# A one-core transformer layer: begun pairs in twos, more of them, and the second value bank in attention

## The chip, the core and the metric

The kernel runs on one core of a Trainium2 chip. The metric is the device time of one execution in microseconds (us); a kernel's time is the median of its runs. The engines are called TensorE (PE in the profile; PEld is its loading of weights), VectorE (DVE), ScalarE (ACT), GpSimd (POOL) and SyncE (SP, which issues DMAs here). SBUF is the memory on the chip that the engines work from; PSUM has eight banks, and matmuls sum into them.

## The reference

One layer of a diffusion backbone over 1024 latent tokens and 256 context tokens, width 1024, all in f32:

```python
x  = x  + 0.5 * ml[2] * swiglu(modulate(rms_norm(x,  norm1_g), ml[0], ml[1]), ffn1_w_in, ffn1_w_out)
cx = cx + 0.5 * mc[2] * swiglu(modulate(rms_norm(cx, norm1_g), mc[0], mc[1]), ffn1_w_in, ffn1_w_out)
hx, hc = modulate(rms_norm(x, norm2_g), ml[3], ml[4]), modulate(rms_norm(cx, norm2_g), mc[3], mc[4])
bg, cg, vc, q, k, v, gt = split(hx @ w_in)          # and the same of hc, for its keys and values
y_conv = bg * short_conv(cg * vc, conv_w)
o = attention(rope(rms_norm(q)), concat(k_ctx, rope(rms_norm(k))), concat(v_ctx, v))   # 8 heads, 2 for keys
x = x + ml[5] * (sigmoid(gt0) * (y_conv @ w_bc) + sigmoid(gt1) * (o @ w_ba)) @ w_out
x = x + 0.5 * ml[8] * swiglu(modulate(rms_norm(x, norm3_g), ml[6], ml[7]), ffn2_w_in, ffn2_w_out)
return rms_norm(x, final_g)
```

## The kernel before

**Precision.** Each f32 operand is split into a high part (a cast to fp32r by ScalarE) and a low part (the rest, a subtraction on VectorE). A product of two operands is three matmuls: high by high, high by low, low by high. `terms` issues these three for one of four blocks of the sum, `k`.

**Products by seven.** The big projections are done by the class `Winograd`. A pair of column blocks of the weights against the two halves of the tokens (`C0`, the first 512, and `C1`, the second 512) would take eight products of half-size blocks; seven products of sums of blocks suffice. Each product is 4 × 3 = 12 matmuls of 128x512, so a pair takes 84. The left factors are sums of weight blocks (made by GpSimd, tiles `sum`, or taken as fetched, tiles `raw`), split into tiles `wl` or `wh`. The right factors `r1` to `r7` are sums of the normalized input, each in four blocks `k`; `norm0` makes `r1` and `r2`, which need `C0` only, and `norm1` makes `r3` to `r7`, which need the normalized `C1`. The results are collected by VectorE in tiles `u`, `v`, `c` and `b`.

**Pairs begun ahead.** While `norm1` works, only products 1 and 2 can run. `start` therefore begins the first `n_ahead` pairs with these two products. For each pair it fetches a bank for product 1, has ScalarE copy the bank to `u`, runs one step of `norm1`, takes a second bank for product 2, and has VectorE add `u` and that bank into `c`. Then `put_aside` lets SyncE write `u` and `c` (tile `uc`, 512 KB) to DRAM (`ucd`). Later `fetch` brings them back one pair ahead, and `second` and `third` continue the pair with products 6, 7, 4, 5 and 3. The left factors of begun pairs are fetched first, all of them in front of those of the products that continue; the left blocks of a begun pair are fetched again later for its sums. Pairs that are not begun do all seven products in a row. Two stages use `start`: `mix`, the projection by `w_in` (20 pairs, `AH2` of them begun), and `fast`, the first matmul of the last FFN (22 pairs, `AH3` begun). The first FFN has a start of its own.

**Attention.** A `Unit` is one head with one half of the tokens; the 16 units alternate `C0` and `C1`. `scores` makes, for each of four blocks of 128 queries, the scores against 256 context keys and 2 × 512 latent keys; VectorE takes the maxima, ScalarE the exponentials. While the next unit's scores are made, `seconds` turns this unit's weights (`turn`, on TensorE) and sums the values (`values`, ten blocks of keys, 30 matmuls into one bank); at the end ScalarE copies the bank to `q` (`output`). Between them, matmuls of the convolution branch and of the merge fill in.

**Banks.** PSUM is given out by three rings: `ps_s` of five banks for products, scores and the rest, `ps_t` of two for transposes, and `ps_o` of one, which in attention holds the value sums. A bank comes free when all that read the tile before it have done so.

**Order.** The code is written in the order of its data, and a scheduler, which models the engines, decides in what order the instructions of each engine stand; an engine then works through its list in order. Each instruction waits for the ones that it depends on. All are issued by one helper, so the profile names line L90 for nearly all, and the tiles' names (with buffer numbers left out) tell them apart.

Of the kernel before, what the change touches and what calls it, by code (L numbers as in the profile page):

```python
# [9 lines left out]
F32 = mybir.dt.float32  # L10
# [8 lines left out]
P = 128  # L19
# [16 lines left out]
C0, C1, CC = ("l", 0, 512), ("l", 512, 512), ("c", 0, CT)  # L36

A_BUFS = 38
W_BUFS = 4
# [4 lines left out]
WAIT = 4  # L44
AH1, BY_HALF, WARM = 13, 8, 32
TOKENS_AT = 5
RESIDENT, AH2, AH3 = 2, 9, 9
SLOT = 1024


# [1 line left out]
def tile_dit_layer(  # L52
# [44 lines left out]
    act, dve, pool, pe, sp = (Engine(e) for e in (nc.scalar, nc.vector, nc.gpsimd, nc.tensor, nc.sync))  # L97
# [3 lines left out]
    wpool = ctx.enter_context(tc.tile_pool(name="wpool", bufs=5))  # L101
# [7 lines left out]
    def uniq(s):  # L109
        n_tiles[0] += 1  # L110
        return f"{s}_{n_tiles[0]}"
# [11 lines left out]
    def ps_s(n=512):  # L123
        return psum.tile([P, 512], F32, tag="s", name=uniq("ps"), bufs=5)[:, :n]
# [4 lines left out]
    def ps_o(n=512):  # L129
        return psum.tile([P, 512], F32, tag="o", name=uniq("po"), bufs=1)[:, :n]  # L130

    def matmul(out, w, x, start, stop, pinned=False, on=False):

        inst = pe.matmul(out, w, x, start=start, stop=stop, skip_group_check=on)
        if pinned:
            tc.keep_in_program_order(inst)
# [329 lines left out]
    def run(steps, n=None):  # L466

        if n is None:
            for _ in steps:
                pass  # L470
        else:
            for _ in range(n):
                next(steps, None)
# [18 lines left out]
    class Winograd:  # L492
# [192 lines left out]
            self.prefetch(4)  # L685
            return self.ready.pop(0)

        def terms(self, ps, w, i, k):
            r = self.r[i][k]
            wh, wl = (w[:, v, k * P : (k + 1) * P] for v in range(2))  # L690
            matmul(ps, wh, r[:, 0], start=k == 0, stop=False)
            matmul(ps, wh, r[:, 1], start=False, stop=False)
            matmul(ps, wl, r[:, 0], start=False, stop=k == 3)

        def product(self, i):
            w, ps = self.left(), ps_s()
# [12 lines left out]

        def start(self, norm):  # L710

            for i in range(self.n_ahead):
                t = wpool.tile([P, 2, 512], F32, tag="wh", name=uniq("uc"), bufs=W_BUFS)
                u, c = t[:, 0], t[:, 1]
                act.copy(out=u, in_=self.product(1))
                run(norm, 1)
                dve.tensor_add(out=c, in0=u, in1=self.product(2))
                self.put_aside(t)
            run(norm)
            self.fetch()  # L720

# [369 lines left out]
    for k in range(4):  # L1091
        if k % 2:
            half1.shifted(h0[k][:, 0], k, xh[k])
        else:
            dve.tensor_scalar(
                out=h0[k][:, 0], in0=xh[k], scalar1=gain1["l"][:, k : k + 1], scalar2=modl[:, k : k + 1],
# [3 lines left out]
    start = half1.start_by_half()  # L1100
# [58 lines left out]
    steps = all_later_mods()  # L1159
# [66 lines left out]
    for j in range(NH):  # L1226
        half1.side = side(j) if j >= SIDE_FROM else None
        u, c = half1.next_first()
# [117 lines left out]
    for i in range(KD):  # L1346
        u = atile("u")
# [5 lines left out]
        for ch, bg, gc in mixed():  # L1353
# [4 lines left out]
            for j in (0, 2):  # L1358
# [3 lines left out]
                    out=ya, in0=u[:, a + j - 1 : b + j - 1], scalar=col(f"w{j}", i), in1=ya, op0=ALU.mult, op1=ALU.add  # L1362
# [207 lines left out]
    class Unit:  # L1570
# [45 lines left out]

        def values(self, kt, pts):
            if kt == 0:
                self.po = ps_o()
            po = self.po  # L1620
            vh, vl = (v[:, self.g * HD : (self.g + 1) * HD] for v in v_tile(kt))
            matmul(po, vh, pts[:, 0], start=(kt == 0), stop=False)
            matmul(po, vh, pts[:, 1], start=False, stop=False)
            matmul(po, vl, pts[:, 0], start=False, stop=(kt == 9))
# [63 lines left out]
    u = units[0]  # L1688
# [57 lines left out]
    for ch in (C0, C1):  # L1746
        o = ch[1]
        for d in range(KD):
            w = load_cols(w_out[0], d * P)
            load(xs(d, ch), xd[d, :, o : o + 512])  # L1750
            ps = ps_s()
# [4 lines left out]
                out=xs(d, ch), in0=ps, scalar=modl[:, 40 + d : 41 + d], in1=xs(d, ch), op0=ALU.mult, op1=ALU.add  # L1756
# [12 lines left out]
        out=gf[:], in0=cols[:, voff["gf"] : voff["gf"] + 8], scalar1=math.sqrt(D), scalar2=None, op0=ALU.mult  # L1769
# [133 lines left out]
```

## Time and profile before

| what | value |
|---|---|
| median of three runs | 2644.59 us (2644.15 to 2645.6) |
| the profiled execution | 2648.45 us |
| its span in the profile | 2646.7 us, mean granted clock of TensorE 0.994 |
| TensorE busy | 2620.2 us, 99% of the span, 12,665 matmuls and transposes |
| VectorE busy | 2019.7 us, 76% |
| ScalarE busy | 1173.9 us, 44% |
| GpSimd busy | 549.7 us, 21% |
| `mix` begins, on TensorE | 879.24 us |
| attention | about 1456 to 1854 us |
| `fast` continues its first pair | about 2037 us |

The profile comes from one execution, and its times are counted from the start of its span. A line of the timeline gives the start of a group of like instructions, the time that it takes, engine, line, operation, output and inputs, shapes and count, and in brackets how long the engine stood idle before it and which instruction ended that. A line of a window gives its length, then the busy time of TensorE, its weight loads, VectorE, ScalarE and GpSimd with the number of instructions in brackets, then the granted clock of TensorE as a share of full speed, the share of DMA engines in use, and GB/s. Matmul ends are modelled, so that starts are the surer times.

### The profile page before, as it was taken

The numbers are of one execution on the slowest core, as the hardware profiler recorded it, in microseconds if no ns is written. First come the engines' busy times: TensorE is split into PE (matmuls) and PEld (weight loads), VectorE is DVE, ScalarE is ACT, GpSimd is POOL, SyncE is SP. The second block draws the span as 40 slices with busy tenths as digits, with TensorE's granted clock in tenths as the row PEclk, the third lists the DMA queues.
The fourth block names the chain that finished last, engine by engine and source line by source line (L and its number), as shares of the span: only waits on it lengthen the run. The fifth ranks groups of instructions, "written<-read, shape, count | busy, mean of one in ns | idle before, by whom it ended". The sixth has DMA issues, their size and how long they took to land.

```text
span 2646.7 us, 35358 instructions
## 1 busy us (share of the span) xinstructions
PE 2620.2 (99%) x12665; PEld 2180.4 (82%) x12665; DVE 2019.7 (76%) x3382; ACT 1173.9 (44%) x2321; POOL 549.7 (21%) x425
## 2 busy tenths in 40 slices
PE   8999999999999999999999999999999999999998
PEld 6888898888888777888888888888887888888888
DVE  5888876888897898877788676685457876666996
ACT  6533454433554632333355576674235333334553
POOL 0144101221010044332023112141001442321100
PEclk9999999999999999999999999999999999999999
DMA  8666465335973455242522532123525542327831
GB/s 322 203 211 195 140 214 168 113 120 204 319 170 115 136 171 169 98 133 78 204 73 91 88 88 64 33 49 105 161 81 178 185 155 86 98 76 281 197 84 64
DMA packets 367018, 378.40 MB, mean 143 GB/s; under 512 B 19431, under 2 KB 252025, under 8 KB 366841
## 3 DMA queue, kind: packets, MB, share of 16 engines
q1 hardware_dynamic: 357400, 357.22, 41.7%
q0 software_dynamic: 9440, 18.91, 4.3%
q8 instruction: 99, 1.62, 0.3%
q14 instruction: 79, 0.64, 0.1%
HBM read 306.26 MB, written 69.76 MB: 142 GB/s over the span
## 4 chain that ended last, share of the span: by engine, by line
PE 59%; DVE 2%; ACT 1%; issue 1%; DMA 0%; POOL 0%; SPq 0%; DVEq 0%; ACTq 0%; POOLq 0%
PE ps L90 49%; PE po L90 5%; PE pt L90 5%; DVE xb L90 0%; DVE y L90 0%; DVE r L90 0%; DMA c<-ucd 0%; DVE wl L90 0%; DVE rs_t L90 0%; ACT r L90 0%; DVE wc L90 0%; ACT pts L90 0%; POOL sum L90 0%; DVE pts L90 0%; ACT q L90 0%
## 5 line engine op out<-in xcount | busy, mean ns | idle before, releaser
L90 PE MATMUL ps<-r,wl 128*128 128x512 f32 x5196 | 1208.1, 392 | 10.8 <-DVE r L90 4.8
L90 PEld LDWEIGHTS ps<-r,wl 128*128 128x128 f32 x5196 | 976.0, 189 | 220.7 <-DVE r L90 6.7
L90 ACT CAST wl<-raw 128x512 fp32r<-128x512 f32 x287 | 177.7, 619 | 235.9 <-PE ps L90 189.2
L90 ACT CAST wl<-sum 128x512 fp32r<-128x512 f32 x218 | 134.2, 620 | 301.5 <-PE ps L90 244.9
L90 DVE TENSOR_TENSOR wl<-raw,wl 128x512 fp32r<-128x512 f32 x287 | 209.3, 731 | 62.2 <-ACT wl L90 60.8
L90 POOL TENSOR_TENSOR sum<-raw 128x512 f32<-128x512 f32 x55 | 81.0, 1472 | 657.1 <-DMA raw<-in_w_in_dram 208.5
L90 DVE TENSOR_TENSOR wl<-sum,wl 128x512 fp32r<-128x512 f32 x218 | 194.6, 894 | 23.2 <-ACT wl L90 22.0
L90 DVE TENSOR_TENSOR u<-u,ps 128x512 f32<-128x512 f32 x186 | 126.1, 679 | 39.2 <-PE ps L90 39.1
L90 DVE SCALAR_TENSOR_TENSOR macc<-rawm,silu_c,macc 128x512 f32<-128x512 f32 x178 | 144.5, 830 | 10.3 <-DMA rawm<-in_w_mod_dram 9.9
L90 POOL TENSOR_TENSOR sum<-raw,sum 128x512 f32<-128x512 f32 x55 | 79.0, 1437 | 323.5 <-DVE wl L90 318.0
L90 ACT CAST rh<-hid 128x512 fp32r<-128x512 f32 x132 | 82.0, 622 | 135.2 <-PE ps L90 108.1
L90 DVE TENSOR_TENSOR pts<-pt,pts 128x512 fp32r<-128x512 f32 x160 | 108.6, 686 | 42.5 <-ACT pts L90 40.6
L90 ACT CAST pts<-pt 128x512 fp32r<-128x512 f32 x160 | 93.3, 594 | 86.3 <-PE pt L90 82.6
L90 DVE TENSOR_REDUCE m<-ps 128x1 f32<-128x512 f32 (+1 forms) x192 | 110.2, 594 | 24.3 <-PE ps L90 20.1
L90 PE MATMUL ps<-rh,wl 128*128 128x512 f32 x360 | 122.8, 390 | 0.0
L90 PE MATMUL ps<-wh,r 128*128 128x512 f32 x384 | 120.7, 392 | 0.0
L90 ACT CAST wh<-raw 128x512 fp32r<-128x512 f32 (+1 forms) x85 | 68.0, 801 | 101.3 <-PE ps L90 79.2
L90 DVE TENSOR_TENSOR rl<-hid,rh 128x512 fp32r<-128x512 f32 x132 | 89.9, 684 | 27.0 <-ACT rh L90 18.2
L90 PE MATMUL po<-pts,vh 128*128 128x512 f32 x256 | 110.0, 435 | 0.2 <-ACT pts L90 0.2
L90 PE MATMUL ps<-kl,qs 128*128 128x512 f32 x384 | 104.1, 395 | 0.0
L90 PE MATMUL ps<-rh,wh 128*128 128x512 f32 x300 | 102.8, 389 | 0.0
L90 PE MATMUL ps<-y,wc 128*128 128x512 f32 x384 | 97.1, 392 | 0.2 <-DVE g L90 0.2
(318 smaller groups left out, 5080.8 us busy)
## 6 DMA issues: line engine op xcount, KB each, us to landing
raw<-in_ffn_w_in_dram SPq DMA_DIRECT2D x130, 512.0 KB
raw<-in_ffn_w_out_dram SPq DMA_DIRECT2D x72, 512.0 KB
raw<-in_w_in_dram SPq DMA_DIRECT2D x61, 512.0 KB
rawm<-in_w_mod_dram SPq DMA_DIRECT2D x104, 256.0 KB
hid<-hd SPq DMA_DIRECT2D x40, 512.0 KB
rawm<-in_w_mod_dram SPq DMA_DIRECT2D x32, 512.0 KB
ucd<-uc SPq DMA_DIRECT2D x29, 512.0 KB
ws<-in_ffn_w_out_dram POOLq DMA_DIRECT2D x26, 512.0 KB, 6.4
```

Source lines behind the costliest of these rows:

```text
L90: inst = getattr(self.engine, name)(*args, **kw)
```

## The change

There are three edits.

1. Twelve pairs are begun ahead in `mix` instead of nine, ten in `fast` instead of nine.
2. `start` begins pairs by twos. It takes the four left factors of two pairs and one bank for each, runs product 1 of both, has ScalarE copy both banks to `u`, and then runs product 2 into the same banks without clearing them (`begins=False`), so that a bank then holds the sum of both products. ScalarE copies that to `c`. The addition on VectorE is gone. In the first group of a stage the terms of both pairs are issued in turn for each `k`; in the others one chain follows the other.
3. In attention a unit of `C1` takes the bank of its value sums from `ps_s`, a unit of `C0` from `ps_o` as before.

```diff
-RESIDENT, AH2, AH3 = 2, 9, 9
+RESIDENT, AH2, AH3 = 2, 12, 10
...
-        def terms(self, ps, w, i, k):
+        def terms(self, ps, w, i, k, begins=True):
             r = self.r[i][k]
             wh, wl = (w[:, v, k * P : (k + 1) * P] for v in range(2))
-            matmul(ps, wh, r[:, 0], start=k == 0, stop=False)
-            matmul(ps, wh, r[:, 1], start=False, stop=False)
-            matmul(ps, wl, r[:, 0], start=False, stop=k == 3)
+            matmul(ps, wh, r[:, 0], start=begins and k == 0, stop=False, on=not begins)
+            matmul(ps, wh, r[:, 1], start=False, stop=False, on=not begins)
+            matmul(ps, wl, r[:, 0], start=False, stop=k == 3, on=not begins)
...
         def start(self, norm):
 
-            for i in range(self.n_ahead):
-                t = wpool.tile([P, 2, 512], F32, tag="wh", name=uniq("uc"), bufs=W_BUFS)
-                u, c = t[:, 0], t[:, 1]
-                act.copy(out=u, in_=self.product(1))
-                run(norm, 1)
-                dve.tensor_add(out=c, in0=u, in1=self.product(2))
-                self.put_aside(t)
+            for j in range(0, self.n_ahead, 2):
+                n = min(2, self.n_ahead - j)
+                self.prefetch(2 * n)
+                ws, ps = [self.ready.pop(0) for _ in range(2 * n)], [ps_s() for _ in range(n)]
+                ts = [wpool.tile([P, 2, 512], F32, tag="wh", name=uniq("uc"), bufs=W_BUFS) for _ in range(n)]
+                for i in (1, 2):
+                    steps = [(k, e) for k in range(4) for e in range(n)]
+                    for k, e in steps if j == 0 else sorted(steps, key=lambda s: s[1]):
+                        self.terms(ps[e], ws[2 * e + i - 1], i, k, i == 1)
+                    for e in range(n):
+                        act.copy(out=ts[e][:, i - 1], in_=ps[e])
+                    if i == 1:
+                        run(norm, n)
+                for t in ts:
+                    self.put_aside(t)
             run(norm)
             self.fetch()
...
         def values(self, kt, pts):
             if kt == 0:
-                self.po = ps_o()
+                self.po = ps_s() if self.ch == C1 else ps_o()
             po = self.po
```

The number of matmuls is the same. Three places show what moves; the names end in the tile's numbers, which differ between the kernels, and the part after the arrow is what is read.

TensorE where `mix` begins, before (`ps_1469`, `ps_1480` are product 1 of pairs 0 and 1, `ps_1476`, `ps_1484` product 2; `r1_1428` to `r1_1431` are the four blocks of `r1`, `r2_1442` on those of `r2`):

```order
L90 MATMUL ps_1469_8296<-r1_1428_8048,wl_1463_8281 128x512 x3
L90 MATMUL ps_1469_8296<-r1_1429_8053,wl_1463_8281 128x512 x3
L90 MATMUL ps_1469_8296<-r1_1430_8058,wl_1463_8281 128x512
L90 MATMUL ps_1476_8334<-r2_1442_8145,wl_1464_8284 128x512
L90 MATMUL ps_1480_8354<-r1_1428_8048,wl_1466_8289 128x512 x3
L90 MATMUL ps_1480_8354<-r1_1429_8053,wl_1466_8289 128x512 x3
L90 MATMUL ps_1480_8354<-r1_1430_8058,wl_1466_8289 128x512
L90 MATMUL ps_1469_8296<-r1_1430_8058,wl_1463_8281 128x512 x2
L90 MATMUL ps_1469_8296<-r1_1431_8063,wl_1463_8281 128x512
L90 MATMUL ps_1480_8354<-r1_1430_8058,wl_1466_8289 128x512 x2
L90 MATMUL ps_1480_8354<-r1_1431_8063,wl_1466_8289 128x512
L90 MATMUL ps_1484_8378<-r2_1442_8145,wl_1467_8292 128x512
```

The same place now, from the last block of product 1 on (`ps_1468` is the bank of pair 0, `ps_1469` that of pair 1):

```order
L90 MATMUL ps_1468_8295<-r1_1431_8063,wl_1463_8281 128x512
L90 MATMUL ps_1469_8296<-r1_1431_8063,wl_1466_8289 128x512
L90 MATMUL ps_1468_8295<-r1_1431_8063,wl_1463_8281 128x512 x2
L90 MATMUL ps_1469_8296<-r1_1431_8063,wl_1466_8289 128x512 x2
L90 MATMUL ps_1468_8295<-r2_1442_8145,wl_1464_8284 128x512 x3
L90 MATMUL ps_1468_8295<-r2_1443_8150,wl_1464_8284 128x512 x3
L90 MATMUL ps_1468_8295<-r2_1444_8155,wl_1464_8284 128x512 x3
L90 MATMUL ps_1468_8295<-r2_1445_8160,wl_1464_8284 128x512
L90 MATMUL ps_1485_8395<-r1_1428_8048,wl_1480_8381 128x512 x2
L90 MATMUL ps_1468_8295<-r2_1445_8160,wl_1464_8284 128x512 x2
L90 MATMUL ps_1469_8296<-r2_1442_8145,wl_1467_8292 128x512 x3
L90 MATMUL ps_1469_8296<-r2_1443_8150,wl_1467_8292 128x512 x3
```

Before, the two products of two pairs stood mixed in four banks. Now the blocks of product 1 of both pairs stand in front (the rows ahead of these read `r1_1428` to `r1_1430`), and product 2 of pair 0 follows into the bank that product 1 left.

TensorE at the end of the begun pairs in `mix`, before (`ps_1575` is the last begun product 2; `ps_1591`, `ps_1593`, `ps_1599`, `ps_1601` are products 6, 7, 4 and 5 of pair 0):

```order
L90 MATMUL ps_1575_8768<-r2_1445_8160,wl_1562_8702 128x512 x3
L90 MATMUL ps_1591_8806<-r6_1499_8439,wl_1568_8728 128x512 x2
L90 MATMUL ps_1593_8824<-r7_1497_8433,wl_1572_8748 128x512 x2
L90 MATMUL ps_1599_8850<-r4_1500_8443,wl_1574_8765 128x512 x2
L90 MATMUL ps_1601_8867<-r5_1498_8436,wl_1590_8803 128x512 x2
L90 MATMUL ps_1591_8806<-r6_1499_8439,wl_1568_8728 128x512
L90 MATMUL ps_1591_8806<-r6_1516_8506,wl_1568_8728 128x512 x3
L90 MATMUL ps_1591_8806<-r6_1533_8573,wl_1568_8728 128x512 x3
L90 MATMUL ps_1593_8824<-r7_1497_8433,wl_1572_8748 128x512
L90 MATMUL ps_1593_8824<-r7_1514_8500,wl_1572_8748 128x512 x3
L90 MATMUL ps_1593_8824<-r7_1531_8567,wl_1572_8748 128x512 x3
L90 MATMUL ps_1599_8850<-r4_1500_8443,wl_1574_8765 128x512
```

The same place now (`ps_1574` is product 2 of the twelfth pair, `ps_1600` and `ps_1602` are products 6 and 7 of pair 0):

```order
L90 MATMUL ps_1574_8812<-r2_1444_8155,wl_1572_8808 128x512 x3
L90 MATMUL ps_1574_8812<-r2_1445_8160,wl_1572_8808 128x512 x3
L90 MATMUL ps_1600_8911<-r6_1499_8452,wl_1596_8899 128x512 x2
L90 MATMUL ps_1602_8929<-r7_1497_8446,wl_1597_8902 128x512 x2
L90 MATMUL ps_1600_8911<-r6_1499_8452,wl_1596_8899 128x512
L90 MATMUL ps_1600_8911<-r6_1509_8480,wl_1596_8899 128x512 x3
L90 MATMUL ps_1600_8911<-r6_1531_8584,wl_1596_8899 128x512 x3
L90 MATMUL ps_1600_8911<-r6_1539_8606,wl_1596_8899 128x512 x3
```

Before, the four products of pair 0 stood mixed, their first blocks in front, and came after nine pairs. Now product 6 runs whole behind twelve pairs, with two matmuls of product 7 among it.

TensorE in attention at the end of a `C0` unit's values, before (`po_2420` is that unit's bank, `po_2479` the next unit's, of `C1`; `vc`, `vh`, `vl` are parts of the values, `pt` are turned weights, `ps_2458` scores):

```order
L90 MATMUL po_2420_13509<-pts_2453_13652,vl_2068_11534 128x512
L90 MATMUL pt_2469_13719<-ident_75,pl_2403_13429 128x128
L90 MATMUL pt_2469_13719<-ident_75,pl_2415_13485 128x128
L90 MATMUL pt_2469_13719<-ident_75,pl_2427_13541 128x128
L90 MATMUL pt_2469_13719<-ident_75,pl_2447_13620 128x128
L90 MATMUL po_2479_13766<-pts_2466_13696,vc_2069_11535 128x512 x3
L90 MATMUL po_2479_13766<-pts_2468_13710,vc_2069_11535 128x512
```

The same place now (`ps_2476` is the bank of the `C1` unit):

```order
L90 MATMUL po_2417_13518<-pts_2450_13661,vl_2065_11543 128x512
L90 MATMUL pt_2466_13728<-ident_75,pl_2400_13438 128x128
L90 MATMUL pt_2466_13728<-ident_75,pl_2412_13494 128x128
L90 MATMUL pt_2466_13728<-ident_75,pl_2424_13550 128x128
L90 MATMUL pt_2466_13728<-ident_75,pl_2444_13629 128x128
L90 MATMUL ps_2455_13676<-kc_2075_11559,qs_2451_13670 128x256 x2
L90 MATMUL ps_2455_13676<-kc_2075_11559,qs_2452_13671 128x256
L90 MATMUL pt_2474_13767<-ident_75,pl_2400_13438 128x128
L90 MATMUL pt_2474_13767<-ident_75,pl_2412_13494 128x128
L90 MATMUL pt_2474_13767<-ident_75,pl_2424_13550 128x128
L90 MATMUL pt_2474_13767<-ident_75,pl_2444_13629 128x128
L90 MATMUL ps_2476_13775<-pts_2463_13705,vc_2066_11544 128x512 x3
```

The `C1` unit's values now go to a bank of the ring, in which the scores (`ps_2455`, `ps_2479`) stand too, and scores and turns stand in front of its first value matmul.

## The prediction

> **What bounds the kernel now.** I read the page first, then TensorE's waits, then the timeline and the windows around each wait, then the chain.
>
> ```profile
> PE 2620.2 (99%) x12665; PEld 2180.4 (82%) x12665; DVE 2019.7 (76%) x3382; ACT 1173.9 (44%) x2321; POOL 549.7 (21%) x425
> ```
>
> The page's first part: TensorE (PE) is busy 99% of the span, so only its pauses, or a lower granted clock, can be won back while the matmuls stay 12,665. VectorE (DVE) at 76% is an average that hides stages in which it is full.
>
> ```profile
> PE ps L90 <- DVE r L90: 4.8, 5, 2.0
> PE ps L90 <- ACT r L90: 3.8, 4, 1.3
> ...
> PE ps L90 <- DVE wl L90: 2.0, 1, 2.0
> ...
> PE po L90 <- ACT q L90: 1.1, 4, 0.3
> ```
>
> TensorE's waits (sum, times, longest). The first three lines touch the operands `r`, the sums of the normalized input, and the weight parts `wl`; the last is the value bank in attention. Next, the price of one matmul when nothing is late, from the chain of waits:
>
> ```profile
> 1142.79 95.23 PE ps L90 x420
> ```
>
> 95.23/420 = 0.2267 us. With it every stall is priced as elapsed time less matmuls × 0.2267. The timeline of TensorE where the projection stage (`mix`) begins:
>
> ```profile
> 879.24 1.07 PE L90 MATMUL ps<-r,wl 128*128 128x512 f32 x4
> 881.11 0.98 PE L90 MATMUL ps<-r,wl 128*128 128x512 f32 x3 [0.81 <-DVE r L90]
> 883.23 9.60 PE L90 MATMUL ps<-r,wl 128*128 128x512 f32 x41 [1.14 <-ACT r L90]
> 892.66 0.95 PE L90 MATMUL pt<-ones,sq_acc 128*128 128x1 f32 x8
> ```
>
> 892.66 − 879.24 = 13.42 us for 4 + 3 + 41 = 48 matmuls, which take 10.88: **2.5 us lost** while the first operands come. Where the ninth begun pair ends and the pairs are continued:
>
> ```profile
> 937.61 3.63 PE L90 MATMUL ps<-r,wl 128*128 128x512 f32 x15
> 943.22 0.96 PE L90 MATMUL ps<-r,wl 128*128 128x512 f32 x3 [1.98 <-DVE r L90]
> 944.91 34.66 PE L90 MATMUL ps<-r,wl 128*128 128x512 f32 x139 [0.73 <-DVE r L90]
> 979.41 0.50 PE L90 MATMUL pt<-ones,sq_acc 128*128 128x1 f32 x4
> ```
>
> 41.80 us for 157 matmuls (35.59): **6.2 us lost**. And at the next lack of weights:
>
> ```profile
> 994.65 7.94 PE L90 MATMUL ps<-r,wl 128*128 128x512 f32 x33
> 1004.64 47.69 PE L90 MATMUL ps<-r,wl 128*128 128x512 f32 x202 [2.05 <-DVE wl L90]
> 1052.17 0.38 PE L90 MATMUL pt<-ident,rs_y 128*128 128x128 f32 x2
> ```
>
> 57.52 us for 235 (53.27): **4.2 us lost**. Where the last FFN's stage (`fast`) begins:
>
> ```profile
> 2036.72 6.93 PE L90 MATMUL ps<-r,wl 128*128 128x512 f32 x28
> 2044.36 1.25 PE L90 MATMUL ps<-r,wl 128*128 128x512 f32 x3 [0.70 <-ACT r L90]
> 2046.58 10.30 PE L90 MATMUL ps<-r,wl 128*128 128x512 f32 x36 [0.96 <-DVE r L90]
> 2057.50 4.71 PE L90 MATMUL ps<-r,wl 128*128 128x512 f32 x18 [0.62 <-ACT r L90]
> ```
>
> 20.78 us for 67 (15.19): **5.6 us lost**. The losses are larger than the waits named. The granted clock (the third number from the right) says why:
>
> ```profile
> 940.00:960.00 20.00, 17.29 (x63) 13.37 (x62) 16.34 (x18) 7.36 (x16) 10.22 (x7) 0.83 0.41 134
> 1000.00:1020.00 20.00, 17.95 (x73) 14.32 (x72) 16.49 (x21) 5.63 (x10) 10.47 (x8) 0.91 0.60 197
> 2040.00:2050.00 10.00, 8.25 (x25) 4.93 (x24) 8.11 (x12) 8.88 (x16) 3.20 (x3) 0.83 0.60 198
> ```
>
> The clock lost is (1 − 0.83) × 20 = 3.4 us, 0.09 × 20 = 1.8 and 0.17 × 10 = 1.7. Each follows waits of 0.7 to 2.05 us.
>
> So 13.0 us lie at place 1 (`mix`), 5.6 at place 2 (`fast`) and 1.1 in attention: 19.7 us are in play.
>
> **The change, part by part.**
>
> *Twelve pairs begun instead of nine, ten instead of nine.* A begun pair does 24 of its 84 matmuls ahead, 5.44 us. Products 6, 7, 4 and 5 need operands that VectorE makes meanwhile:
>
> ```profile
> 948.24 0.68 DVE L90 TENSOR_TENSOR r<-nt,r 128x512 fp32r<-128x512 f32 x1
> ```
>
> Pair 0's first products are issued by about 939 us (wait at 943.22), the last operands are ready near 949: about 10 us late. Three more pairs move that point 3 × 5.44 = 16.3 us back, while VectorE's work until then does not grow: the operands lead by some 6 us, and the 6.2 us stall goes. (Three pairs bring six weight parts, 6 × 0.68 = 4.1 us, less than the additions that go, below.) What is late next is the weights of pair 0, whose fetch stands on SP's queue behind the last puts-aside; a fetch takes about this long (chain):
>
> ```profile
> 987.59 4.21 DMA c<-ucd
> ```
>
> TensorE's waits named no fetch in these stretches, so the fetches are ahead; I take 0.2 us and keep 0 to 4.2, a whole one. At place 2 the 67 matmuls would have ended at 2036.72 + 15.19 = 2051.9, and the last operand came near 2057.5. One pair more moves the need to 2057.3, and VectorE and ScalarE have the time of the removed additions besides: I leave 0.8 us of the 5.6 and keep 0 to 5.6.
>
> *The sum of products 1 and 2 is made in the bank.* VectorE loses one addition for each begun pair, ScalarE (ACT) gains one copy (and three and one pairs more):
>
> ```profile
> L90 ACT COPY uc<-ps 128x512 f32<-128x512 f32 x31 | 17.8, 586 | 22.0 <-PE ps L90 21.8
> ```
>
> Nine additions, each 0.68 like the addition of the same size quoted above, are 6.1 us that leave a VectorE which is the late engine at place 1; ScalarE takes 24 copies × 0.586 = 14.1 us instead of 5.3 over 65 us, with its 7.36 us of 20 in the window from 940 as the nearest load. That is hidden, except in the first group. There product 2 adds onto the bank only after ScalarE copied it, and ScalarE is full with operands, without a pause, until the copy that before starts at:
>
> ```profile
> 887.42 0.59 ACT L90 COPY uc<-ps 128x512 f32<-128x512 f32 x1
> ```
>
> The first 24 matmuls are done before that; if the copy starts at 887.4 the second 24 start near 888.0 and end at 888.0 + 5.44 = 893.4, where 890.1 would be without loss: 3.3 us instead of 2.5. The wait is then some 2 us in one piece, of the kind that cost clock in three places above. I put half of 1.7 us on it, 0.85 (bounds 0 and 1.7). The wait for the copy stands at the head of TensorE's queue, and behind it wait all later chains; at later groups the second bank's twelve matmuls (2.7 us) cover the copy's 0.59.
>
> [...]
>
> *The stall at 1002.* It came when a weight part met a slow addition:
>
> ```profile
> 1002.84 1.75 DVE L90 TENSOR_TENSOR wl<-sum,wl 128x512 fp32r<-128x512 f32 x1
> ```
>
> Such additions (1.75 instead of 0.68 us) lie beside GpSimd's sums. After the change the pairs come in another phase; nothing removes this for certain, but VectorE enters the pairs without backlog. I leave 0.5 of the 4.2 us, and keep 0 to 4.2.
>
> *What gets worse.* A pair that was whole takes 84 × 0.2267 = 19.0 us, a continued one 60 × 0.2267 = 13.6, with nearly the same work on VectorE. The windows of four pairs, the first two continued, the last two whole:
>
> ```profile
> 1038.60:1052.30 13.70, 13.70 (x63) 11.31 (x62) 13.12 (x17) 3.12 (x5) 4.74 (x4) 1.00 0.42 135
> 1052.30:1066.00 13.70, 13.70 (x63) 11.35 (x62) 13.60 (x21) 3.84 (x7) 4.70 (x3) 1.00 0.60 211
> 1066.00:1085.00 19.00, 19.00 (x85) 15.76 (x84) 17.92 (x25) 7.16 (x12) 7.94 (x5) 1.00 0.40 131
> 1085.00:1104.10 19.10, 19.10 (x86) 15.79 (x86) 12.46 (x20) 6.71 (x12) 5.01 (x4) 1.00 0.25 78
> ```
>
> Continued pairs already fill 13.12 and 13.60 of 13.70 us. The first whole one has 17.92; without two weight parts and one addition (3 × 0.68) it is 15.9 in 13.6, 2.3 us short, and the next has 12.46 − 2.0 = 10.5 and catches up. Part of the shortage lies in work that TensorE doesn't wait for: 0.7 us, from 0 to 4.
>
> Four more pairs also put aside and fetch back 512 KB each and fetch one left part twice, 1.5 MB × 4 = 6 MB. In the windows above DMA is busy 0.25 to 0.60, so it hides; uncovered it would be in the queue wait counted already.
>
> *The value bank in attention.* Eight units take a bank of the ring of five. Before, a unit's first value matmul waited for the copy out of the single bank:
>
> ```profile
> 1498.71 0.59 ACT L90 COPY q<-po 128x512 f32<-128x512 f32 x1
> ...
> 1500.31 0.71 ACT L90 ACTIVATE pl<-ps,nm 128x512 f32<-128x512 f32 x1
> ```
>
> ```profile
> 1499.36 1.18 PE L90 MATMUL po<-pts,vc 128*128 128x512 f32 x4 [0.31 <-ACT q L90]
> ```
>
> The four waits of 1.1 us go, and 1.0 is my value. From above the bound is the stage's whole idle time, 398.00 − 395.95 = 2.05 us:
>
> ```profile
> 1456.00:1854.00 398.00, 395.95 (x2134) 330.34 (x2133) 265.66 (x550) 242.89 (x596) 89.44 (x85) 1.00 0.29 72
> ```
>
> From below it is a ring that runs short: 2 us, three exponentials of the row above (0.71 each).
>
> **Sum.** Place 1: left are 3.3 + 0.85 + 0.2 + 0.5 + 0.7 = 5.5, gain 13.0 − 5.5 = 7.5. Place 2: 5.6 − 0.8 = 4.8. Attention 1.0. Together 13.3 us, 0.50%. The profiled execution, 2648.45 us (span 2646.7), would become 2635.2. It lies 3.9 above the median of 2644.59; the median becomes **2631.3**.
>
> **The rivals.** A measurement of this kernel can tell 0.2%, 5.3 us, from no change.
>
> *Stalls only move.* VectorE, not the operands, is the bound of continued pairs, so its shortage shows at once: the 4.2 us stay, the 4 us of the pairs come in full, the first group takes 3.3 + 1.7: left 13.4 at place 1, gain −0.4; place 2 gives 4.8 and attention 1.0, together 5.4: 2639.2. If place 2 gives half, 2641.6. For it: 13.60 of 13.70. Against it: six additions fewer stand before this stretch, and 10.5 after it.
>
> *Slower: the ring runs dry in attention.* Each of the eight units holds one of five banks through its ten values, while four rounds of scores want two to three banks each. If each of the 8 × 4 = 32 rounds waits for one more exponential, 0.71 us, that is 22.7 us; less 13.3, +9.4: 2654.0. It decides from 13.3/32 = 0.42 us a round. For it: ring banks come free only behind ScalarE's exponentials. Against it: no wait for a `ps` bank is among the waits in attention, ScalarE is busy 242.89 of 398.00, and TensorE idles only 2.05. [...]
>
> *All goes.* Nothing new is late: 19.7 us, 2624.9.
>
> *No effect.* The scheduler already mixed the first two pairs' products, so twos may bring nothing, and the operands are late by something other than place in the order: 2644.6. Against it: the wait at 943.22 names `r`, and 16.3 us of other matmuls come in front of it.
>
> **Chances.** Forecast 0.68, stalls only move 0.20, slower 0.04, all goes 0.06, no effect 0.02. The predicted time is that of the forecast. Its own bounds: 2624.9 with everything gone; with the terms that are most open at their bad ends by half (2 of the 4 us of the pairs, 2 of the 4.2, half the clock, 1.4 at place 2) about 7 us are lost, 2638.3. Eight in ten: 2625.0 to 2640.5, which takes in most of the first rival. Faster by over 0.2% needs under 2639.3: the forecast, all goes, and half of the first rival, 0.84; within 0.2%: the other half and no effect, 0.12; slower 0.04.
>
> **What would show it.** Right: between the first group and pair 4 no wait for `r` longer than 0.3 us, granted clock 1.00 where it was 0.83; no addition `uc<-uc,ps` in these stages; in attention no wait for `ACT q`. The first group is right if it waits about 2 us for the copy `uc<-ps`. Wrong: waits for `DVE wl` after 1000 us with a clock under 0.95 (stalls only move); waits for `ACT pl` or `ACT pc` on `ps` in attention (the ring). The prediction is wrong if the time is over 2640.5, or if place 2 keeps more than 3 us.

## The result, and the profile after

The changed kernel takes **2635.68 us** (median of 6 runs, 2634.84 to 2637.66), the kernel before in the same comparison 2644.97 (6 runs). The ratio is 0.9961, 95% interval 0.9951 to 0.9971: about 9.3 us, 0.35% by the medians, faster. Forecast were 2631.3 us and 13.3 us of gain, range 2625.0 to 2640.5. The time lies inside the range; the gain is 70% of the one forecast. The profiled execution's span fell from 2646.7 to 2635.9 us, by 10.8.

The first part of the page after:

```profile
PE 2613.6 (99%) x12665; PEld 2178.3 (83%) x12665; DVE 1997.9 (76%) x3360; ACT 1180.8 (45%) x2343; POOL 543.7 (21%) x425
```

The count of matmuls is the same; VectorE did 22 instructions fewer and ScalarE 22 more. TensorE's waits (sum, times, longest):

```profile
PE ps L90 <- ACT uc L90: 1.8, 2, 1.1
PE pt L90 <- DVE pts L90: 1.7, 7, 0.4
...
PE ps L90 <- ACT r L90: 1.3, 1, 1.3
PE ps L90 <- ACT pc L90: 0.8, 1, 0.8
...
PE ps L90 <- DVE r L90: 0.4, 1, 0.4
```

`DVE r` fell from 4.8 to 0.4 us, `ACT r` from 3.8 to 1.3, and `ACT q` is gone. New are `ACT uc` (the copy out of the bank), `ACT pc` (an exponential) and, not shown, 0.6 us for `DVE nm`; the wait for `DVE pts` (turned weights in attention) rose from 0.7 to 1.7. Place 1 in TensorE's timeline, from the first matmul of `mix` on:

```profile
881.02 1.52 PE L90 MATMUL ps<-r,wl 128*128 128x512 f32 x6
882.89 0.98 PE L90 MATMUL ps<-r,wl 128*128 128x512 f32 x3 [0.35 <-DVE r L90]
884.81 3.70 PE L90 MATMUL ps<-r,wl 128*128 128x512 f32 x15 [0.94 <-DVE wl L90]
889.65 6.91 PE L90 MATMUL ps<-r,wl 128*128 128x512 f32 x29 [1.14 <-ACT uc L90]
896.40 0.95 PE L90 MATMUL pt<-ones,sq_acc 128*128 128x1 f32 x8
...
904.96 87.09 PE L90 MATMUL ps<-r,wl 128*128 128x512 f32 x383
991.89 0.50 PE L90 MATMUL pt<-ones,sq_acc 128*128 128x1 f32 x4
992.25 68.31 PE L90 MATMUL ps<-r,wl 128*128 128x512 f32 x300
1060.39 0.38 PE L90 MATMUL pt<-ident,rs_y 128*128 128x128 f32 x2
1060.53 19.75 PE L90 MATMUL ps<-r,wl 128*128 128x512 f32 x86
1080.68 4.62 PE L90 MATMUL ps<-r,wl 128*128 128x512 f32 x19 [0.40 <-DVE wl L90]
```

The first group: 53 matmuls from 881.02 to 896.40, 15.38 us against 53 × 0.2267 = 12.01, so 3.4 us are lost. From 904.96 to 1080 there is no stop: the 300 matmuls behind 992.25 take 1060.39 − 992.25 = 68.14 us, 300 × 0.2267 = 68.01. The stalls that stood at 943 and 1002 are both gone, and only 0.40 us is waited for in a later continued pair. The windows say the same of the clock (third number from the right), and give attention as a whole in the last line:

```profile
880.00:900.00 20.00, 17.57 (x79) 13.65 (x78) 15.68 (x34) 14.21 (x27) 0.00 (x0) 1.00 0.59 195
1000.00:1020.00 20.00, 20.00 (x90) 16.57 (x89) 19.90 (x31) 6.31 (x11) 7.29 (x5) 1.00 0.41 135
1070.00:1090.00 20.00, 19.60 (x87) 15.90 (x86) 20.00 (x28) 5.82 (x10) 7.29 (x5) 1.00 0.52 165
1435.00:1855.00 420.00, 416.68 (x2229) 347.58 (x2229) 275.23 (x571) 251.22 (x615) 89.45 (x85) 1.00 0.26 76
```

The clock is 1.00 in all, also from 1000 us on, where it was 0.91 before. VectorE is at 20.00 of 20.00 in the stretch with the 0.40 wait. In attention TensorE is idle 420.00 − 416.68 = 3.32 us; a window of the same length in the profile before was

```profile
1440.00:1860.00 420.00, 417.76 (x2236) 348.30 (x2235) 278.87 (x573) 252.13 (x615) 89.72 (x86) 1.00 0.30 76
```

2.24 us. Attention became 1.1 us worse by these windows. They match only to about 2 us (the first scores start at 1432.5 us now and at 1439.9 before); a window of the changed kernel from 1432 on has 3.58 us idle, 1.3 us more than before. Place 2:

```profile
2000.27 19.54 PE L90 MATMUL ps<-r,wl 128*128 128x512 f32 x85
2020.52 39.77 PE L90 MATMUL ps<-r,wl 128*128 128x512 f32 x174 [0.70 <-ACT uc L90]
```

85 matmuls take 19.27 us and had 2020.52 − 2000.27 = 20.25, so 1.0 us is lost, around one wait of 0.70 for the copy.

### The profile page after: what moved, and what is told of

It reads as the page before. It is cut to its first block, busy times and chain, and to the rows that moved or that the text cites. A ratio compares the mean times of both kernels' runs of the same rounds, so it can differ in the third digit from the quotient of the medians.

```text
span 2635.9 us, 35385 instructions
## 1 busy us (share of the span) xinstructions
PE 2613.6 (99%) x12665; PEld 2178.3 (83%) x12665; DVE 1997.9 (76%) x3360; ACT 1180.8 (45%) x2343; POOL 543.7 (21%) x425
## 4 chain that ended last, share of the span: by engine, by line
PE 93%; DVE 3%; ACT 1%; DMA 1%; issue 1%; SPq 0%; POOL 0%; DVEq 0%; ACTq 0%
PE ps L90 80%; PE pt L90 8%; PE po L90 6%; DMA rawm<-in_w_mod_dram 1%; DVE wl L90 0%; DVE xb L90 0%; DVE macc L90 0%; DVE m L90 0%; DVE y L90 0%; ACT x L90 0%; DVE pts L90 0%; ACT r L90 0%; DMA hd<-u 0%; DMA mcol<-mrow 0%; ACT wl L90 0%
## 5 line engine op out<-in xcount | busy, mean ns | idle before, releaser
L90 DVE TENSOR_REDUCE m<-ps 128x1 f32<-128x256 f32 (+1 forms) x192 | 110.9, 596 | 29.7 <-PE ps L90 28.8
L90 POOL TENSOR_TENSOR sum<-sum,raw 128x512 f32<-128x512 f32 x55 | 88.2, 1603 | 5.6 <-PE ps L90 3.9
```

What stands on the lines that cost most here:

```text
L90: inst = getattr(self.engine, name)(*args, **kw)
```

## The experiments

Each is one kernel against the kernel before on the same chip; the ratio is its time over that kernel's. Beside its time stands what TensorE lost by place in its profiled execution: the sum, over all matmul starts, of the time to the next start beyond the median for that kind of matmul (512 columns: 227 ns). By this measure the kernel before lost 2.7, 6.4, 4.3 and 6.2 us where the prediction's rows gave 2.5, 6.2, 4.2 and 5.6. "First group" is the start of `mix`, "pair 0" the stretch where the begun pairs end and pair 0 is continued, "later pairs" what follows it in `mix`, "place 2" the start of `fast`. "Attention" is TensorE's idle time in a window of 420 us (– where none was read).

| kernel | us (before on that chip) | ratio, 95% interval | first group | pair 0 | later pairs | place 2 | attention |
|---|---|---|---|---|---|---|---|
| before | 2644.97 | | 2.7 | 6.4 | 4.3 | 6.2 | 2.24 |
| changed | 2635.68 (2644.97) | 0.9961, 0.9951 to 0.9971 | 3.5 | 0.0 | 0.8 | 1.1 | 3.32 |
| ahead_only | 2637.07 (2646.68) | 0.9960, 0.9946 to 0.9973 | 2.7 | 0.0 | 1.7 | 2.6 | – |
| twos_only | 2643.12 (2646.68) | 0.9986, 0.9978 to 0.9995 | 3.5 | 7.2 | 0.5 | 3.9 | – |
| bank_only | 2648.06 (2646.68) | 1.0005, 0.9996 to 1.0014 | 2.7 | 4.5 | 4.5 | 6.2 | 3.32 |
| no_bank | 2635.95 (2646.68) | 0.9959, 0.9946 to 0.9971 | 3.5 | 0.0 | 1.3 | 1.1 | 3.60 |
| ahead_10 | 2640.92 (2647.60) | 0.9977, 0.9967 to 0.9986 | 3.5 | 2.5 | 5.0 | 1.1 | – |
| ahead_14 | 2636.07 (2647.60) | 0.9960, 0.9947 to 0.9972 | 3.5 | 0.0 | 1.2 | 1.1 | – |
| first_four_banks | 2636.44 (2647.60) | 0.9961, 0.9949 to 0.9974 | 2.0 | 0.0 | 0.7 | 3.1 | – |
| add_on_vector | 2639.30 (2647.60) | 0.9969, 0.9958 to 0.9981 | 2.0 | 0.9 | 2.8 | 2.7 | – |
| four_in_mix | 2633.11 (2646.69) | 0.9950, 0.9937 to 0.9962 | 2.0 | 0.0 | 0.5 | 1.1 | – |
| ring_all | 2649.47 (2646.69) | 1.0012, 1.0003 to 1.0021 | 2.7 | 5.3 | 2.1 | 6.2 | 4.63 |
| ring_six | 2656.60 (2646.69) | 1.0038, 1.0025 to 1.0050 | 3.5 | 1.0 | 1.4 | 2.8 | 11.61 |
| ring_six_four | 2655.88 (2646.69) | 1.0033, 1.0021 to 1.0046 | 2.0 | 0.7 | 1.3 | 2.6 | – |

One execution's figures carry noise. `bank_only` and `ring_all`, whose order in `mix` is that of the kernel before, lost 4.5 and 5.3 us at pair 0 where it lost 6.4, and 4.5 and 2.1 in the later pairs where it lost 4.3. In these two columns a difference of a microsecond or two therefore shows nothing unless a wait in the trace goes with it. The first group and place 2 agree in these three kernels.

### Which part brings the gain: the number of pairs, or the sum in the bank

`ahead_only` is the kernel before with one line changed:

```diff
-RESIDENT, AH2, AH3 = 2, 9, 9
+RESIDENT, AH2, AH3 = 2, 12, 10
```

> Twelve and ten begun pairs, begun one by one with VectorE's addition as before, value bank as before. Theory A (the number of begun pairs is what removes the stalls at places 1 and 2): three pairs move the need back by 16.3 us against operands 10 us late, so the 6.2 and most of the 5.6 us go whatever becomes of the additions, and the phase of the pairs shifts as in the changed kernel: 9 to 13 us faster than before, 2632 to 2636 us. Theory B (the sum in the bank, which frees VectorE, removes them): VectorE has three more additions and six more weight parts, the waits for r stay: 2641 to 2646 us.

Measured: 0.9960, as fast as the whole change. TensorE in place 1 (timeline):

```profile
901.91 82.78 PE L90 MATMUL ps<-r,wl 128*128 128x512 f32 x364
```

82.78 us for 364 matmuls, 364 × 0.2267 = 82.5: no stop, where before there were two waits for `r` (1.98 and 0.73 us) and 6.83 us at a granted clock of 0.50, from 944.17 us on. The additions on VectorE were all there. It lost more than `no_bank` only in the later pairs (1.7 against 1.3) and at place 2 (2.6 against 1.1), where TensorE waited for a weight part:

```profile
2041.26 12.05 PE L90 MATMUL ps<-r,wl 128*128 128x512 f32 x50 [1.19 <-ACT wl L90]
```

`twos_only` is the changed kernel with `AH2, AH3 = 9, 9` and the value bank as before.

> Nine begun pairs in both stages, begun by twos with the sum in the bank, value bank as before. Theory A: the need stays where it was, VectorE saves 6.1 us of the 10 us by which the operands are late; at place 1 about half of the 6.2 us goes, at place 2 about half of the 5.6, the first group costs 0.9 more: 2639 to 2643 us. Theory B: the 6.1 us suffice and all stalls go: 2632 to 2636 us. In the trace the wait for r at pair 0 is there by A and gone by B.

Measured: 0.9986, 3.6 us faster by the medians, inside theory A's range of 2 to 6. The stall at pair 0 did not shrink. It was named otherwise, though:

```profile
938.46 42.76 PE L90 MATMUL ps<-r,wl 128*128 128x512 f32 x180 [4.31 <-ACT wl L90]
```

TensorE waits for the weight part `wl`, 4.31 us, not for `r` as theory A had it. ScalarE's timeline at that place says what `wl` waited for:

```profile
934.71 0.62 ACT L90 CAST r<-nt 128x512 fp32r<-128x512 f32 x1 [3.63 <-DVE nt L90]
...
937.79 1.14 ACT L90 CAST wl<-sum 128x512 fp32r<-128x512 f32 x2
```

The casts of `wl` at 937.79 stand in ScalarE's list behind five casts of `r` and a copy, and the first of these waits 3.63 us for `nt`, the last block of `norm1` from VectorE. In the kernel before, the first casts of pair 0's `wl` (`wl<-sum`) start at 930.19, ahead of those of `r`. The operands themselves did come earlier. The last one, made at 948.24 before, is made at 942.55 here, with `mix` beginning at the same time:

```profile
942.55 0.68 DVE L90 TENSOR_TENSOR r<-nt,r 128x512 fp32r<-128x512 f32 x1
```

So VectorE had 6.1 us less to do and the operands came 5.7 us earlier, but that won nothing at pair 0, because TensorE waited there for a weight part in another engine's list. Theory A holds in that the sum in the bank alone does not remove the stall; its number for place 1 (half gone) was wrong. Whether the relief would have removed it with the casts of `wl` in front, as before, was not tested.

### Where the count of pairs saturates

`ahead_10` and `ahead_14` are `no_bank` (below) with 10 and 10, and with 14 and 12 pairs:

```diff
-RESIDENT, AH2, AH3 = 2, 12, 10
+RESIDENT, AH2, AH3 = 2, 10, 10
```

> The changed kernel with the single value bank (no_bank) and ten begun pairs in the first stage instead of twelve, ten in the last as before. Theory A (need against operands): with nine pairs by twos TensorE lost 7.2 us where pair 0 starts; one more pair moves the need back by 5.4, so about 1.8 us (0 to 3) are lost there, and some clock if the wait is over 1.9 us in one piece: 2636 to 2640 us, 1 to 4 slower than no_bank. If instead the last two pairs did nothing (the sum in the bank and a single further pair are enough): the same as no_bank, 2636 us.

Measured: 0.9977, 1.8 per mille or 4.8 us slower than `no_bank` by the ratios, a little over the 1 to 4 expected. TensorE's timeline:

```profile
1005.48 4.83 PE L90 MATMUL ps<-r,wl 128*128 128x512 f32 x13 [2.04 <-DVE wl L90]
```

Around pair 0 2.5 us are lost, 1.8 were expected. What had not been expected is the wait of 2.04 us at 1005, behind which the granted clock was 0.50 from 1006.80 to 1010.21 us: the stall that stood at 1002 before is back, ended by a weight part from VectorE. With twelve pairs it does not come.

> no_bank with fourteen and twelve begun pairs. Theory A: VectorE stood idle 7.2 us before pair 0 of the changed kernel, so the operands already lead with twelve; two more pairs win nothing at place 1, at most the 1.1 us that are left at place 2, and two more pairs become continued ones of 13.6 us, in which VectorE is full: 0 to 3 us slower than no_bank. A rival by which every further begun pair brings about the same (10 us / 3 pairs): 5 us faster than no_bank.

Measured: 0.9960, the same as with twelve, and 0.0, 1.2 and 1.1 us lost at pair 0, in the later pairs and at place 2. The rival, by which every pair brings as much, is out. VectorE's timeline of the changed kernel shows why: with twelve pairs the operands already lead.

```profile
942.61 0.69 DVE L90 TENSOR_TENSOR r<-nt,r 128x512 fp32r<-128x512 f32 x1
950.47 1.30 DVE L90 TENSOR_TENSOR wl<-sum,wl 128x512 fp32r<-128x512 f32 x2 [7.17 <-ACT wl L90]
```

The last operand is ready at 943.3; then VectorE stands idle 7.17 us before the weights of pair 0 come.

### The sum in the bank, and its price in the first group

`add_on_vector` takes from `no_bank` the sum in the bank: product 2 has a bank of its own, and VectorE adds.

```diff
+                    if i == 2:
+                        ps = [ps_s() for _ in range(n)]
...
-                        self.terms(ps[e], ws[2 * e + i - 1], i, k, i == 1)
+                        self.terms(ps[e], ws[2 * e + i - 1], i, k)
...
-                        act.copy(out=ts[e][:, i - 1], in_=ps[e])
+                        if i == 1:
+                            act.copy(out=ts[e][:, 0], in_=ps[e])
+                        else:
+                            dve.tensor_add(out=ts[e][:, 1], in0=ts[e][:, 0], in1=ps[e])
```

> no_bank, but in all groups product 2 has banks of its own and VectorE adds the copy and the bank: pairs by twos without the sum in the bank. ahead_only lost 2.6 us at place 2 where no_bank lost 1.1, and 1.7 against 1.3 in the later pairs of place 1. If the additions on VectorE cost that: 2 to 3 us lost at place 2 and 1.5 to 2.5 later at place 1, about 1 to 2 us slower than no_bank. If the order by twos brings it: 1.1 and 1.3 as in no_bank, and the first group better by 0.8.

Measured: 0.9969 against 0.9959 for `no_bank`; the intervals overlap, so the time alone does not part them. The places do: 2.8 against 1.3 us in the later pairs, 2.7 against 1.1 at place 2, as the first theory had it, and the first group better by 1.5. TensorE's waits in the first 250 us of the stage:

```profile
PE ps L90 <- DVE wl L90: 3.3, 4, 1.0
```

Weight parts from VectorE are late four times; in `no_bank` they are late twice, by 1.8 us in all. So by the places, in pairs begun by twos, the sum in the bank takes 0.9 + 1.5 + 1.6 = 4.0 us off and costs 1.5 in the first group, 2.5 us net. The ratios differ by 0.0010, which is 2.6 us, but with overlapping intervals that is no proof of its own. Against pairs begun one by one with additions (`ahead_only`: 2.7, 0.0, 1.7, 2.6) the whole of the edit brings 1.1 us, which the times (0.9960 and 0.9959) don't show. `first_four_banks` gives only the first group of each stage its own banks (`own = i == 2 and j == 0`).

> no_bank, but in the first group of each stage product 2 has banks of its own and VectorE adds, as before; all other groups sum in the bank. If the wait for ScalarE's copy is what makes the first group lose 3.5 us instead of 2.7: 0.8 us less lost at place 1, no wait for ACT uc there, other places unchanged; in time 0.8 faster than no_bank, which the runs can hardly tell. If the operands are what it waits for: 3.5 us lost as before.

Measured: 0.9961. The first group lost 2.0 instead of 3.5, almost twice the gain that was expected, so the copy was what it waited for. Place 2 got worse by 2.0 us: TensorE there, and ScalarE's list at that time:

```profile
2034.51 1.67 PE L90 MATMUL ps<-r,wl 128*128 128x512 f32 x6 [2.12 <-ACT uc L90]
```

```profile
2030.75 0.63 ACT L90 ACTIVATE c<-c 128x512 f32<-128x512 f32 x1 [1.55 <-DMA c<-ucd]
...
2033.88 1.06 ACT L90 COPY uc<-ps 128x512 f32<-128x512 f32 x2
```

The copy stands behind an activation that waited 1.55 us for a block put aside to come back, and behind casts. `four_in_mix` therefore does it in the first stage alone (the same edit on the changed kernel, `own = i == 2 and j == 0 and self.plain`).

> The changed kernel, but in the first group of the projection stage alone product 2 has banks of its own and VectorE adds; the last FFN sums in the bank throughout. first_four_banks lost 2.0 us instead of 3.5 in that group, and 3.1 instead of 1.1 at place 2, where it waited 2.1 us for ACT uc. If these two belong to their own stages, 1.5 us is won at place 1 and place 2 stays at 1.1: 1.5 us faster than the changed kernel, the fastest version so far. If the wait at place 2 moves with the phase of the whole kernel, it is there again.

Measured: 2633.11 us, 0.9950, the fastest of all. Its interval overlaps that of the changed kernel, so what the first group is worth is read from the places: 2.0 us lost there instead of 3.5, and 1.1 at place 2 as in the changed kernel, without the wait of `first_four_banks`. In its timeline the 60 matmuls from 880.25 to 895.73 take 15.48 us, 13.60 without loss, and the wait for `ACT uc` is not there:

```profile
880.25 1.52 PE L90 MATMUL ps<-r,wl 128*128 128x512 f32 x6
882.12 0.96 PE L90 MATMUL ps<-r,wl 128*128 128x512 f32 x3 [0.35 <-DVE r L90]
884.04 11.85 PE L90 MATMUL ps<-r,wl 128*128 128x512 f32 x51 [0.96 <-DVE wl L90]
895.73 0.95 PE L90 MATMUL pt<-ones,sq_acc 128*128 128x1 f32 x8
```

### The value bank in attention

`bank_only` is the kernel before with the one line of attention changed; `no_bank` the changed kernel with that line undone.

```diff
-                self.po = ps_o()
+                self.po = ps_s() if self.ch == C1 else ps_o()
```

> The kernel before with the C1 units' values in the ring, nothing else. In the trace of the changed kernel TensorE's idle time in the 398 us of attention is 3.32 us instead of 2.05. Theory C (the ring is short where a C1 unit starts, and the turns wait longer for VectorE): 1 to 2.5 us slower than before, 2646 to 2647.5 us, with a wait for the exponentials (ACT pc) on a ps bank. Theory D (the difference is chance, the four waits for the copy that go are the net effect): 2643.5 to 2644.5 us, 1 us faster.

Measured: 1.0005, interval 0.9996 to 1.0014; the time alone excludes neither theory. TensorE's waits in attention and the window:

```profile
PE pt L90 <- DVE pts L90: 1.7, 7, 0.4
PE ps L90 <- ACT pc L90: 0.8, 1, 0.8
```

```profile
1440.00:1860.00 420.00, 416.68 (x2229) 347.56 (x2228) 274.83 (x571) 251.25 (x616) 89.49 (x85) 1.00 0.29 75
```

3.32 us idle instead of 2.24, with the very waits of the changed kernel (1.7 and 0.8). So with nine begun pairs this line alone costs the 1.1 us, and the wait for `ACT pc` that C asked for is there; but the larger part is turned weights, `pts`, coming late from VectorE. The line also moves the order: from 1499 to 1841 us the matmuls stand otherwise than in the kernel before.

> The changed kernel with all value sums in the single bank as before. Theory C: 1 to 2.5 us faster than the changed kernel, 2633 to 2635 us, TensorE idle 2.05 us in attention. Theory D: 1 us slower than the changed kernel, 2636.5 to 2637 us. Places 1 and 2 as in the changed kernel by both.

Measured: 0.9959, neither theory's number: no difference from the changed kernel. The waits for `ACT q` are back (1.1 us), and two new ones stand in attention. TensorE:

```profile
1518.91 0.50 PE L90 MATMUL po<-pts,vh 128*128 128x512 f32 x1 [0.59 <-ACT pts L90]
...
1528.73 0.50 PE L90 MATMUL ps<-kl,qs 128*128 128x512 f32 x1 [1.00 <-ACT pc L90]
```

ScalarE just before the second of them:

```profile
1526.07 0.62 ACT L90 CAST y<-y 128x512 fp32r<-128x512 f32 x1 [0.49 <-DMA y<-yd]
```

and the issue of that fetch on SyncE (min, median and max of eight, in ns):

```profile
L90 SPq DMA_DIRECT2D y<-yd x8: 387/605/6448, 1512.1 to 1522.5; - x8
```

One issue of `y<-yd` stood 6448 ns in SyncE's queue, a fetch came late, ScalarE waited 0.49 us for it, and the exponential behind it let TensorE wait 1.00. The order of the matmuls in attention is that of the kernel before. The long issue goes with the begun pairs and the order together: the longest takes 6.2 to 7.2 us in all six kernels with more begun pairs and the single value bank, 2.7 and 3.7 in the changed kernel and `four_in_mix`, and at most 0.7 in the four kernels with nine pairs. What holds it was not found.

The stage's time goes the same way. From the matmul ahead of the first value sum in attention to one behind the last, 2,027 matmuls, TensorE took 375.8 us in the kernel before and in `twos_only`. With more begun pairs and the same order it took 377.4 to 378.2 in all six kernels. With the line changed it took 377.4, with nine pairs (`bank_only`) as with twelve (the changed kernel, `four_in_mix`). So the line alone costs about 1.6 us here, the further pairs alone cost 1.6 to 2.4, and both together no more than one of them. That is why undoing the line wins nothing.

`ring_all` is the kernel before with `self.po = ps_s()` for all units.

> The kernel before with the value sums of all sixteen units in the ring, so that a bank of the five is held throughout attention. Theory C (a ring short of one bank costs in attention; with eight units it cost 1.0 us of TensorE's starts, 11.5 against 10.5): with sixteen units there is no unit left that relieves it, 2 to 6 us more lost in attention than before, waits for ACT pc and ACT pl on ps banks, 0.1 to 0.2% slower than before. Theory D (the ring has room, the 1.0 us was order and chance): 0 to 1 us more than before.

Measured: 1.0012, slower, and idle 4.63 us: 2.4 more than before, as C had it for the amount. Not for the waits:

```profile
1440.00:1860.00 420.00, 415.37 (x2220) 346.45 (x2219) 274.14 (x568) 249.90 (x614) 89.51 (x85) 1.00 0.28 74
```

```profile
PE pt L90 <- DVE pts L90: 2.3, 5, 0.6
...
PE ps L90 <- ACT pc L90: 0.3, 1, 0.3
```

`ACT pc` is 0.3 us; `DVE pts` is 2.3. `ring_six` gives the changed kernel one ring of six in place of five and one.

```diff
-        return psum.tile([P, 512], F32, tag="s", name=uniq("ps"), bufs=5)[:, :n]
+        return psum.tile([P, 512], F32, tag="s", name=uniq("ps"), bufs=6)[:, :n]
...
-        return psum.tile([P, 512], F32, tag="o", name=uniq("po"), bufs=1)[:, :n]
+        return psum.tile([P, 512], F32, tag="s", name=uniq("po"), bufs=6)[:, :n]
```

> The changed kernel with one ring of six banks for scores, products and values instead of five and one, all units in it; the order on TensorE changes in other places too. Theory C: in attention neither the copy nor the ring is waited for, 9 to 10.5 us lost instead of 12.0, about 2 us faster than the changed kernel if the other stages stay. Theory D: as in the changed kernel, 12 us lost in attention, since the single bank and the ring's are only named otherwise.

Measured: 1.0038, slower than the kernel before and than the changed one. Attention's window and waits:

```profile
1448.00:1868.00 420.00, 408.39 (x2160) 334.01 (x2159) 271.01 (x558) 244.14 (x603) 89.61 (x85) 1.00 0.26 71
```

```profile
PE pt L90 <- DVE pts L90: 4.7, 12, 1.0
PE po L90 <- ACT pts L90: 3.0, 4, 1.7
```

11.61 us idle in a ring that is one bank larger: theory C, that the ring is short of a bank, falls as a full account. TensorE waits for turned weights here too, 4.7 + 3.0 us. The scheduler orders attention anew with other rings, and the waits follow the order. Whether what the line costs comes from the bank or from the order that it led to stays open. `ring_six_four` puts both edits together.

> ring_six and four_in_mix together: by their sum 1.5 us less lost in the first group and 2 us less in attention, 3.5 us faster than the changed kernel. If the ring of six is worse in other stages, slower than four_in_mix.

Measured: 1.0033, slower than `four_in_mix`. The first group's 1.5 us are there, the rest is as in `ring_six`, whose largest loss lies in attention and not, as the expectation feared, in other stages.

## Why the prediction was right, point by point

*Pair 0.* Right, for the reason given: three more pairs move the need behind the operands. Forecast 0.2 us left, measured 0.0. `ahead_only` shows that the further pairs alone do it, and `twos_only` that the relief of VectorE alone, in the order that it led to, does not. The lead was a little larger than the 6 us worked out: pair 0 starts at about 951 us, 7.7 after the last operand.

*The stall at 1002.* 0.5 left was forecast, 0.1 is measured. That this would go was a guess about phase; `ahead_10`, where it returns with its 2.04 us, shows that it was one.

*Continued pairs.* 0.7 us forecast, 0.8 measured, with VectorE full in just that stretch; so close a match is luck, given the noise of these figures. The rival "stalls only move" did not happen with twelve pairs; with ten it did in part.

*First group.* 3.3 us forecast, 3.4 measured, but the parts differ. The copy costs 1.5 us, as `first_four_banks` shows, where the forecast gave it 0.8; in return the operands and weight parts, with both pairs' product 1 in front, cost 2.0 instead of 2.7. That the total fits is in part luck. The wait for the copy was to be some 2 us in one piece; it was 1.14. The clock term, 0.85, was 0: the waits came in pieces of 0.35, 0.94 and 1.14 us, and the clock stayed at 1.00. ScalarE's list shows the copy straight behind the last cast of an operand:

```profile
889.02 0.57 ACT L90 COPY uc<-ps 128x512 f32<-128x512 f32 x1
```

*Place 2.* 0.8 left forecast, 1.0 measured. It took both causes that the forecast named: with the further pair alone (`ahead_only`) 2.6 us were left, with the sum in the bank alone (`twos_only`) 3.9.

*Attention.* This step failed: "the four waits of 1.1 us go, and 1.0 is my value". They went, and more than 2 us of other waits came (`pts`, `pc`, `nm`); the loss of 1.1 lies inside the bound from below that was kept. What I left out is that the change also moves the order: the turns stand where VectorE has not finished. I also left out that further begun pairs cost time in attention by themselves, 1.6 to 2.4 us in six kernels. The slower rival, in which every round waits 0.71 us, did not happen: there was one wait of 0.8.

*The sum.* By the table place 1 gave 13.4 − 4.3 = 9.1 us (7.5 forecast), place 2 5.1 (4.8), attention −1.1 (+1.0): 13.1, next to 13.3. The span fell by only 10.8. Timed between the same matmuls of both traces, the part from the first matmul of `mix` to the first value sum won 9.1 us (594.6 to 585.5), the stretch of attention above lost 1.6 (375.8 to 377.4), and all behind it won 5.0. What lies ahead of `mix` lost 1.8, but no instruction was moved there, and the 12 executions with that order begin `mix` anywhere from 877.4 to 881.0 us.

The median fell by 9.3, 4.0 less than forecast. Attention took 2.1 of these. Besides, the losses were read from an execution 3.9 us above its kernel's median, and the gain was then taken off the median. Its mean granted clock was 0.994; the 50 executions of this kernel beside the experiments had 0.995 to 0.999. `bank_only` and `ring_all`, with the same order in `mix`, took 592.8 and 591.2 us for the 594.6 and had 3.4 us at half clock there instead of 10.2. So some 2 to 3 of the 9.1 us belong to that execution, with its clock as the likely cause, and not to the change; that the table's sum came so near to 13.3 is luck.

## What to carry to other kernels

Where an engine pauses for operands that another one is making, count the work that can be put in front of the need and compare it with the lateness: two numbers from the timeline gave most of the gain here, and beyond the point where the lead is positive more work brings nothing. Relief for the engine that is late helps only where the waiting engine asks next for what comes earlier: in `twos_only` the operands came 5.7 us earlier, and TensorE stood waiting for a weight part. Read a loss from more than one execution before you forecast its end, above all where the granted clock is part of it. When a buffer is moved to another ring, price the new order, not only the wait that it removes: look at who stands in front of whom in each engine's list.

## What the runs showed of the hardware

A wait of about 2 us did not always cost clock. After 2.04 us in `ahead_10` and after 4.31 us in `twos_only` the granted clock was 0.5 for 3.4 us; after 2.04 us in `add_on_vector` and 1.65 in `twos_only` it stayed at 1.00. In the kernel before it was 0.50 for 6.83 us from 944.17 us on, behind a wait of 1.98 us and with one of 0.73 at its start, for 3.41 us from 1005.61 on, behind one of 2.05, and for 3.41 us from 2046.67 on, behind waits of 0.70 and 0.96. First `ahead_10`, with the wait in the upper row (3.41 − 1.37 = 2.04 us idle):

```profile
1003.39:1006.80 3.41, 1.37 (x7) 1.10 (x7) 3.41 (x5) 1.14 (x2) 1.50 (x1) 1.00 0.21 80
1006.80:1010.21 3.41, 3.41 (x10) 2.65 (x9) 3.41 (x5) 1.14 (x2) 1.28 (x1) 0.50 0.70 235
```

Then `add_on_vector`, from the end of a wait of the same length on:

```profile
2042.00:2049.00 7.00, 7.00 (x30) 5.35 (x31) 6.94 (x11) 2.59 (x5) 1.68 (x1) 1.00 0.49 165
```

So a wait of 2.04 us was followed by another 1.7 us of loss (half of 3.41) in one execution and by none in the other; what decides between them was not shown. The 1.9 us at which the expectation for `ahead_10` lets a wait in one piece cost clock were my estimate: they lie between the 1.65 us of `twos_only` and the 1.98 of the kernel before, and `add_on_vector` waited longer without that loss. The clock is also part of the noise at pair 0: `bank_only`, with the order of the kernel before, waited 2.04 and 0.71 us there, was granted 1.00 from 942 to 949 us and lost 4.5 us; the kernel before waited 1.98 and 0.73, was granted 0.58 from 943 to 950 and lost 6.4. In `ring_six` the granted clock was 1.00 in attention over all its short idles, 11.61 us in 420.
